# A two-layer encoder trunk on one core: which engine turns which quarter of x behind a border, and the first quarter and first weight unit in two parts

## Chip, core and metric

One core of one Trainium2 chip runs the whole kernel. The metric is the device time of one execution in microseconds, lower is better. TensorE (PE) multiplies and writes to PSUM; Vector (DVE), Scalar (ACT) and GpSimd (POOL) do the elementwise work; SyncE (SP) issues the loads.

## What is computed

Two layers on 256 tokens of width 2048 in float32: a token mixer of four head groups with one input projection `w_in` and one output projection `w_out`, and a SwiGLU with a hidden width of 5632. Each half has an RMSNorm before and behind it:

```python
def rmsnorm(x, g):
    xf = x.astype(jnp.float32)
    y = xf * lax.rsqrt(jnp.mean(xf * xf, axis=-1, keepdims=True) + EPS)
    return (y * g.astype(jnp.float32)).astype(x.dtype)

def reference(x, norm_mix_pre, ..., ffn_gate, ffn_up, ffn_down):
    split_at = np.cumsum(SPLIT_SIZES)[:-1].tolist()
    for l in range(DEPTH):
        h = rmsnorm(x, norm_mix_pre[l])
        proj = h @ w_in[l]
        a_q, a_k, a_v, b_glu, c_q, c_k, c_v, d_q, d_k, d_v = jnp.split(proj, split_at, axis=-1)
        out_a = diff_attention(a_q, a_k, a_v, diff_lambda[l], diff_subln[l], l)
        out_b = conformer_conv(b_glu, conv_dw[l], conv_dw_b[l], conv_ln_g[l], conv_ln_b[l],
                               conv_pw[l], conv_pw_b[l])
        out_c = gqa_axial_attention(c_q, c_k, c_v, gqa_q_norm[l], gqa_k_norm[l])
        out_d = neighbourhood_attention(d_q, d_k, d_v, na_rpb[l])
        mixed = jnp.concatenate([out_a, out_b, out_c, out_d], axis=-1) @ w_out[l]
        x = x + rmsnorm(mixed, norm_mix_post[l])
        h = rmsnorm(x, norm_ffn_pre[l])
        f = (jax.nn.silu(h @ ffn_gate[l]) * (h @ ffn_up[l])) @ ffn_down[l]
        x = x + rmsnorm(f, norm_ffn_post[l])
    return x
```

## The kernel before

**Products.** The 256 tokens are two halves, `tok` 0 and 1, of 128. Each projection runs over its output columns in pairs of 512-column banks and over its contraction in blocks `k` of 128 rows; for `w_in`, gate and up there are 16. One block of weights for one pair, 128x1024, is a unit. A float32 product is made of three products in a rounded format: Scalar makes the rounded high part of a unit (`whi`, `split_hi`, L222), Vector the low part, the rest (`wlo`, `split_lo`, L231), with the norm's gain taken in. The same holds for x: `xT` has a high and a low part. `products` (L297) issues, for one unit and one token half, high x high and high x low for each of the two banks, and then low x high for both: six matmuls of 512 columns. The low part of x is so needed with the fifth.

**Order.** `plan` (L261) lays the steps of a pair in groups of units; a group runs for token half 0 and then for half 1. The first pair behind a border has `FIRST` (L46), groups of 6, 5 and 5 units, the first pair of all has `START`, 2, 2, 4, 4, 4. Seven high and seven low parts may be alive (`NSPLIT`, L38), three loads of two units each (`NRAW`). The whole order is written by the program itself when it is built: `run` (L345) walks the steps, and `tick` (L318) moves generators on by one `yield` when an estimated clock of the engines says that what they wait for is done. Each engine then takes its instructions in that order.

**x at a border.** When the last bank of `w_out` or `ffn_down` is done for a token half, `post` (L494) makes the new x of that half with Vector, 512 columns (a quarter) at a time: `new_x(c)`. The next projection needs x turned: quarter `c` of x gives `xT[c]`, the blocks `k` = 4c to 4c + 3. Quarters 0 to 2 are turned by TensorE (`transpose_x`, L421): four transposes of 128x128 into one PSUM bank (`tp`, of which there are two), a high part by Scalar, a low part by Vector (`split_hi_lo`, L194). Quarter 3 is turned by Vector (L531 to L542) with 16 transposes of 32 rows by 128, in four batches with a `yield` behind each, into `xt`, from which Scalar and Vector make the parts. There are three such borders: into gate and up of layer 0, into `w_in` of layer 1, into gate and up of layer 1. At the start `first_x` (L463) has TensorE turn all quarters as they are loaded.

## Time and profile before

| | |
|---|---|
| median of 3 runs | 2178.41 us (2178.34 to 2178.55) |
| the profiled execution | 2178.1 us |
| its span in the trace | 2175.9 us |
| TensorE matmuls busy | 2154.6 us, 99% |
| Vector busy | 1300.2 us, 60% |
| Scalar busy | 1092.4 us, 50% |
| DMA | 206 GB/s mean |

The span is what the trace shows of the execution; the time has some 2 us around it. A record of a matmul is longer than its share of time, since matmuls are pipelined: the distance of two starts is the pace. Bracketed at the end of a row of the timeline is the idle time of that engine before the row and who ended it.

### The profile page before, as it was taken

The page shows a single profiled execution, that of the slowest core. Times are in us where ns is not written, and L with a number is a line of the kernel's source. Part 1 is how long each engine was busy: PE and PEld are TensorE (multiplying, and loading weights), DVE is VectorE, ACT ScalarE, POOL GpSimd, SP SyncE. Part 2 cuts the span into 40 slices and gives each one's busy share as a digit, 9 for nine tenths or more (in the row PEclk, how much of TensorE's full clock was granted, in tenths as well). Part 3 has the DMA queues.
Part 4 walks back from the last instruction along what each step waited for, and adds up shares of the span by engine and source line. Part 5 has one row for each costly group of instructions (what it writes and reads, how often), then busy time and mean ns, then how long its engine had stood idle before and what let it go on. Part 6 is the DMA issues. An engine that isn't in the chain of part 4 may idle for free.

```text
span 2175.9 us, 25246 instructions
## 1 busy us (share of the span) xinstructions
PE 2154.6 (99%) x9696; PEld 1778.7 (82%) x9696; DVE 1300.2 (60%) x1616; ACT 1092.4 (50%) x1398; POOL 29.9 (1%) x38
## 2 busy tenths in 40 slices
PE   8999999999999999999999999999999999999998
PEld 7888888888888888888878888888888888888886
DVE  5898556755546554444488974566555555454444
ACT  6656755544445444343455577555444444443432
POOL 0000000000000000000000000000000000000000
PEclk9999999999999999999999999999999999999999
DMA  7556446776776666655565563557667666665553
GB/s 277 194 176 185 170 148 223 232 219 210 225 217 220 209 226 216 220 193 193 208 225 187 193 192 136 199 188 251 213 222 223 211 215 222 222 213 213 193 219 130
DMA packets 200281, 447.52 MB, mean 206 GB/s; under 512 B 20704, under 2 KB 43744, under 8 KB 197856
## 3 DMA queue, kind: packets, MB, share of 16 engines
q1 hardware_dynamic: 200016, 445.87, 60.9%
q8 instruction: 76, 1.25, 0.2%
q14 instruction: 45, 0.37, 0.1%
q10 hardware_dynamic: 144, 0.03, 0.0%
HBM read 425.93 MB, written 19.92 MB: 205 GB/s over the span
## 4 chain that ended last, share of the span: by engine, by line
PE 95%; ACT 2%; DVE 1%; issue 1%; DMA 1%; DVEq 0%; POOLq 0%; ACTq 0%; SPq 0%
PE acc L89 91%; PE tp L89 3%; PE sc L89 1%; ACT whi L89 1%; DVE wlo L89 1%; ACT workA L89 0%; DMA lc<-in_heads_dram 0%; ACT L89 0%; DVE mx L89 0%; ACT xT L89 0%; DVE xt L89 0%; DMA x<-in_x_dram 0%; ACT conv L89 0%; ACT junk L89 0%; DVE xT L89 0%
## 5 line engine op out<-in xcount | busy, mean ns | idle before, releaser
L89 PE MATMUL acc<-whi,xT 128*128 128x512 f32 x4096 | 1292.7, 393 | 5.4 <-ACT xT L89 2.4
L89 PEld LDWEIGHTS acc<-whi,xT 128*128 128x128 f32 x4096 | 770.0, 188 | 169.5 <-ACT xT L89 3.5
L89 PE MATMUL acc<-wlo,xT 128*128 128x512 f32 x2048 | 799.4, 390 | 2.6 <-DVE wlo L89 2.6
L89 ACT ACTIVATE whi<-raw,gains 128x1024 fp32r<-128x1024 f32 x512 | 580.5, 1150 | 365.3 <-PE acc L89 334.3
L89 DVE SCALAR_TENSOR_TENSOR wlo<-raw,gains,whi 128x1024 fp32r<-128x1024 f32 x512 | 641.7, 1278 | 188.9 <-ACT whi L89 180.9
L89 PEld LDWEIGHTS acc<-wlo,xT 128*128 128x128 f32 x2048 | 385.3, 188 | 81.9 <-DVE wlo L89 4.4
L89 DVE TENSOR_TENSOR wlo<-raw,whi 128x1024 fp32r<-128x1024 f32 x240 | 292.6, 1223 | 260.5 <-ACT whi L89 243.8
L89 PE MATMUL acc<-whi,hT 128*128 128x512 f32 x1408 | 434.1, 389 | 0.0
L89 ACT ACTIVATE whi<-raw 128x1024 fp32r<-128x1024 f32 x240 | 253.7, 1061 | 304.1 <-PE acc L89 304.0
L89 PEld LDWEIGHTS acc<-whi,hT 128*128 128x128 f32 x1408 | 264.3, 188 | 55.0
L89 PE MATMUL acc<-wlo,hT 128*128 128x512 f32 x704 | 273.9, 389 | 0.0
L89 PEld LDWEIGHTS acc<-wlo,hT 128*128 128x128 f32 x704 | 132.1, 188 | 27.3
L89 DVE TENSOR_TENSOR hT<-ht,hT 128x1024 fp32r<-128x1024 f32 x22 | 27.0, 1226 | 163.5 <-ACT hT L89 163.5
L89 DVE SCALAR_TENSOR_TENSOR h<-acc,rstd,h 128x512 f32<-128x512 f32 x44 | 33.1, 751 | 113.4 <-ACT h L89 113.4
L89 DVE SCALAR_TENSOR_TENSOR conv<-uT,lc,conv 128x256 f32<-128x256 f32 x240 | 99.4, 481 | 0.0
L89 ACT ACTIVATE hT<-ht 128x1024 fp32r<-128x1024 f32 x22 | 23.3, 1059 | 128.7 <-DMA ht<-h_blocks 128.7
L89 ACT ACTIVATE h<-acc,rstd 128x512 f32<-128x512 f32 x44 | 30.3, 689 | 80.5 <-PE acc L89 80.3
L89 ACT ACTIVATE junk<-acc 128x512 bf16<-128x512 f32 x32 | 19.0, 595 | 55.9 <-PE acc L89 53.0
L89 PE MATMUL acc<-whi,mixC 128*128 128x512 f32 x128 | 44.7, 402 | 0.0
L89 DVE TENSOR_TENSOR mg<-acc,gpost 128x512 f32<-128x512 f32 x32 | 21.3, 686 | 35.8 <-PE acc L89 19.5
L89 PE MATMUL acc<-whi,mixB 128*128 128x512 f32 x128 | 42.2, 397 | 0.0
L89 PE MATMUL acc<-whi,mixD 128*128 128x512 f32 x128 | 41.6, 391 | 0.0
(139 smaller groups left out, 987.4 us busy)
## 6 DMA issues: line engine op xcount, KB each, us to landing
raw<-in_ffn_gate_dram SPq DMA_DIRECT2D x176, 512.0 KB, 3.8
raw<-in_ffn_up_dram SPq DMA_DIRECT2D x176, 512.0 KB, 5.1
raw<-in_ffn_down_dram SPq DMA_DIRECT2D x88, 1024.0 KB, 5.0
raw<-in_w_in_dram SPq DMA_DIRECT2D x63, 1024.0 KB, 5.1
raw<-in_w_out_dram SPq DMA_DIRECT2D x32, 1024.0 KB, 5.0
raw<-in_w_in_dram SPq DMA_DIRECT2D x34, 512.0 KB, 4.7
h_blocks<-blocks SPq DMA_DIRECT2D x44, 256.0 KB, 5.5
ht<-h_blocks SPq DMA_DIRECT2D x88, 128.0 KB, 6.0
```

Source lines behind the costliest of these rows:

```text
L89: return f(*args, **kw)
```

## The change

Four things. In `post` a new number `early` says how many quarters TensorE turns: 2 at a border into gate and up, 4 at the one into `w_in`. The rest, quarters 2 and 3 or none, is turned by Vector in a loop, each when the quarter before is marked; the 16 transposes are now a function `turn`. `transpose_x` takes quarter 0 in two halves with a PSUM bank for each, at the borders and at the start, and so claims both banks. `new_x(0)` is made in two halves of 256 columns. The first unit of all (`index` 0) has its high and its low part made in two pieces of 512 columns.

```diff
@@ -219,6 +219,11 @@
             self.load(self.raws[self.next_raw], between)
             self.next_raw += 1
 
+    @staticmethod
+    def pieces(u):
+
+        return [slice(0, 512), slice(512, 1024)] if u.index == 0 else [slice(0, 1024)]
+
     def split_hi(self, u):
         self.chain = 0.0
         u.hi = self.wp.tile([P, 1024], F32R, tag="hi", name=self.name("whi"))
@@ -226,7 +231,8 @@
         if gain is None:
             self.nc.scalar.activation(u.hi, w, AF.Copy)
         else:
-            self.nc.scalar.activation(u.hi, w, AF.Copy, scale=gain[:, u.k:u.k + 1])
+            for cs in self.pieces(u):
+                self.nc.scalar.activation(u.hi[:, cs], w[:, cs], AF.Copy, scale=gain[:, u.k:u.k + 1])
 
     def split_lo(self, u):
         self.chain = 0.0
@@ -235,9 +241,10 @@
         if gain is None:
             self.nc.vector.tensor_tensor(u.lo, w, hi, op=ALU.subtract)
         else:
-            self.nc.vector.scalar_tensor_tensor(
-                u.lo, w, gain[:, u.k:u.k + 1], hi, op0=ALU.mult, op1=ALU.subtract
-            )
+            for cs in self.pieces(u):
+                self.nc.vector.scalar_tensor_tensor(
+                    u.lo[:, cs], w[:, cs], gain[:, u.k:u.k + 1], hi[:, cs], op0=ALU.mult, op1=ALU.subtract
+                )
 
     def splits_to(self, n, needed):
 
@@ -421,18 +428,24 @@
     def transpose_x(self, phase, tok, c):
 
         nc = self.nc
-        yield from self.claim("tp")
+        halves = 2 if c == 0 else 1
+        n = 4 // halves
+        yield from self.claim("tp", halves)
         if tok == 0:
             self.xT[c] = self.slot([2, 4, S], F32R, "xT")
-        b = self.bank("tp", (4, P))
-        for i in range(4):
-            k = 4 * c + i
-            nc.tensor.transpose(b[:, i], self.x[tok][:, k * P:(k + 1) * P], self.ident)
-        dst = [self.xT[c][:, i, :, tok * P:(tok + 1) * P] for i in range(2)]
-        self.split_hi_lo(dst, b)
+        banks = []
+        for h in range(halves):
+            b = self.bank("tp", (n, P))
+            banks.append(b)
+            for i in range(n):
+                k = 4 * c + h * n + i
+                nc.tensor.transpose(b[:, i], self.x[tok][:, k * P:(k + 1) * P], self.ident)
+        for h, b in enumerate(banks):
+            dst = [self.xT[c][:, i, h * n:(h + 1) * n, tok * P:(tok + 1) * P] for i in range(2)]
+            self.split_hi_lo(dst, b)
         self.mark("x", phase, c, tok)
         yield
-        self.free("tp")
+        self.free("tp", halves)
 
     def x_stats(self, tok):
         for c in range(4):
@@ -514,32 +527,32 @@
                                   self.x[tok][:, c * 512:(c + 1) * 512])
             return
         yield
-        new_x(0)
+        for h in range(2):
+            cs = slice(h * 256, (h + 1) * 256)
+            nc.vector.scalar_tensor_tensor(self.x[tok][:, cs], self.mg[phase, 0][:, tok, cs], r, self.x[tok][:, cs],
+                                           op0=ALU.mult, op1=ALU.add)
         new_x(1)
         then = ("gu", phase[1]) if phase[0] == "out" else ("in", phase[1] + 1)
-        for c in range(3):
-            yield
-            self.spawn(self.transpose_x(then, tok, c))
+        early = 2 if phase[0] == "out" else 4
+        for c in range(4):
+            yield
+            if c < early:
+                self.spawn(self.transpose_x(then, tok, c))
             if c + 2 < 4:
                 new_x(c + 2)
         self.x_stats(tok)
         nc.sync.dma_start(self.xd[rows, :], self.x[tok])
         yield
         self.x_rstd(then, tok)
-        yield
-        yield from self.until(1, "x", then, 2, tok)
-        if tok == 0:
-            self.xT[3] = self.slot([2, 4, S], F32R, "xT")
-        t = self.tmp([4, P], "xt")
-        for q in range(4):
-            qs = slice(32 * q, 32 * q + 32)
-            for r in range(4):
-                rs = slice(32 * r, 32 * r + 32)
-                src = self.x[tok][:, 3 * 512:].rearrange("p (k n) -> p k n", k=4)
-                nc.vector.transpose(t[qs, :, rs], src[rs, :, qs])
-            yield
-        self.split_hi_lo([self.xT[3][:, i, :, tok * P:(tok + 1) * P] for i in range(2)], t)
-        self.mark("x", then, 3, tok)
+        for c in range(early, 4):
+            yield
+            yield from self.until(1, "x", then, c - 1, tok)
+            if tok == 0:
+                self.xT[c] = self.slot([2, 4, S], F32R, "xT")
+            t = self.tmp([4, P], "xt")
+            yield from self.turn(t, self.x[tok][:, c * 512:(c + 1) * 512])
+            self.split_hi_lo([self.xT[c][:, i, :, tok * P:(tok + 1) * P] for i in range(2)], t)
+            self.mark("x", then, c, tok)
 
 
     def ffn_half(self, phase, j, tok):
@@ -575,6 +588,16 @@
         self.split_hi_lo(dst, t.rearrange("p t (k n) -> p k t n", k=4))
         for tok in range(T):
             self.mark("h", l, j, tok)
+
+    def turn(self, dst, src):
+
+        src = src.rearrange("p (k n) -> p k n", n=P)
+        for q in range(4):
+            qs = slice(32 * q, 32 * q + 32)
+            for r in range(4):
+                rs = slice(32 * r, 32 * r + 32)
+                self.nc.vector.transpose(dst[qs, :, rs], src[rs, :, qs])
+            yield
 
 
     def layer_consts(self, l):
```

Vector, border into gate and up of layer 0. `wlo` are low parts of units, 7 to 11 here; `xt_3126` and `xt_3253` are quarter 3 of token halves 0 and 1, one row is a batch of four. Before:

```order
L89 SCALAR_TENSOR_TENSOR wlo_3155<-raw_2983,gains,whi_3132 128x1024
L89 SCALAR_TENSOR_TENSOR wlo_3177<-raw_3009,gains,whi_3153 128x1024
L89 STREAM_TRANSPOSE xt_3126<-x_2742 32x4x32 x4
L89 TENSOR_TENSOR xT_3090<-tp_3189,xT_3090 128x4x128
L89 SCALAR_TENSOR_TENSOR wlo_3198<-raw_3009,gains,whi_3175 128x1024
L89 TENSOR_REDUCE xs_3209<-ssx 128x1
L89 TENSOR_SCALAR ms_3211<-xs_3209 128x1
L89 SCALAR_TENSOR_TENSOR wlo_3216<-raw_3036,gains,whi_3196 128x1024
L89 SCALAR_TENSOR_TENSOR wlo_3226<-raw_3036,gains,whi_3214 128x1024
L89 STREAM_TRANSPOSE xt_3126<-x_2742 32x4x32 x4
L89 STREAM_TRANSPOSE xt_3253<-x_2744 32x4x32 x4
L89 TENSOR_TENSOR xT_3125<-xt_3126,xT_3125 128x4x128
```

Now, where `xt_3165` and `xt_3244` are quarter 2 of token halves 0 and 1, and `xt_3276` is quarter 3 of half 0; the first row is the low part of unit 8:

```order
L89 SCALAR_TENSOR_TENSOR wlo_3172<-raw_3021,gains,whi_3151 128x1024
L89 SCALAR_TENSOR_TENSOR wlo_3191<-raw_3021,gains,whi_3170 128x1024
L89 STREAM_TRANSPOSE xt_3165<-x_2750 32x4x32 x4
L89 SCALAR_TENSOR_TENSOR wlo_3208<-raw_3047,gains,whi_3189 128x1024
L89 SCALAR_TENSOR_TENSOR wlo_3218<-raw_3047,gains,whi_3206 128x1024
L89 TENSOR_REDUCE xs_3229<-ssx 128x1
L89 TENSOR_SCALAR ms_3231<-xs_3229 128x1
L89 STREAM_TRANSPOSE xt_3165<-x_2750 32x4x32 x4
L89 STREAM_TRANSPOSE xt_3244<-x_2752 32x4x32 x4
L89 STREAM_TRANSPOSE xt_3165<-x_2750 32x4x32 x4
L89 STREAM_TRANSPOSE xt_3244<-x_2752 32x4x32 x4
L89 TENSOR_TENSOR xT_3164<-xt_3165,xT_3164 128x4x128
```

Quarter 2 of half 0 has its last two batches behind the low parts of units 10 and 11, about where quarter 3 had its last; quarter 3 starts behind that.

TensorE, the same border: the end of unit 7 and the start of unit 8 (the first of quarter 2) for token half 0. Before:

```order
L89 MATMUL acc_3039<-whi_3132,xT_3047 128x512
L89 MATMUL acc_3040<-whi_3132,xT_3047 128x512
L89 MATMUL acc_3039<-whi_3153,xT_3090 128x512 [waits Activation_49]
L89 MATMUL acc_3039<-wlo_3177,xT_3090 128x512 [waits DVE_49]
L89 MATMUL acc_3040<-whi_3153,xT_3090 128x512
```

Now (`xT_3164` is quarter 2):

```order
L89 MATMUL acc_3050<-whi_3134,xT_3065 128x512
L89 MATMUL acc_3051<-whi_3134,xT_3065 128x512
L89 MATMUL acc_3050<-whi_3151,xT_3164 128x512 [waits Activation_49]
L89 MATMUL acc_3050<-wlo_3172,xT_3164 128x512 [waits DVE_49]
L89 MATMUL acc_3051<-whi_3151,xT_3164 128x512
```

The same product waits for Scalar in both; its `xT` came through TensorE and PSUM before and comes through Vector's `xt` now.

TensorE, border into `w_in` of layer 1: `x_7699` and `x_7701` (now `x_7739` and `x_7741`) are token halves 0 and 1. Before:

```order
L89 MATMUL acc_8057<-whi_8024,xT_8064 128x512
L89 MATMUL tp_8108<-ident,x_7699 128x128 [waits PE_49]
L89 MATMUL tp_8108<-ident,x_7699 128x128 x3
L89 MATMUL acc_8056<-whi_8033,xT_8064 128x512
L89 MATMUL acc_8056<-wlo_8052,xT_8064 128x512
L89 MATMUL acc_8057<-whi_8033,xT_8064 128x512
L89 MATMUL acc_8057<-wlo_8052,xT_8064 128x512
L89 MATMUL acc_8056<-whi_8033,xT_8064 128x512
L89 MATMUL acc_8057<-whi_8033,xT_8064 128x512
L89 MATMUL tp_8127<-ident,x_7701 128x128 [waits DMAHW6_49,DVE_49,PE_49]
L89 MATMUL tp_8127<-ident,x_7701 128x128 x3
L89 MATMUL acc_8134<-whi_7917,xT_8016 128x512 [waits Activation_49]
```

Now:

```order
L89 MATMUL acc_8100<-whi_8077,xT_8114 128x512
L89 MATMUL tp_8159<-ident,x_7739 128x128 [waits PE_49]
L89 MATMUL tp_8159<-ident,x_7739 128x128 x3
L89 MATMUL tp_8167<-ident,x_7739 128x128 [waits PE_49]
L89 MATMUL tp_8167<-ident,x_7739 128x128 x3
L89 MATMUL tp_8180<-ident,x_7741 128x128 [waits DMAHW6_49,DVE_49]
L89 MATMUL tp_8180<-ident,x_7741 128x128
L89 MATMUL tp_8183<-ident,x_7741 128x128 [waits DVE_49]
L89 MATMUL tp_8183<-ident,x_7741 128x128
L89 MATMUL acc_8190<-whi_7957,xT_8057 128x512 [waits Activation_49]
```

Quarters 2 and 3 of half 0 and quarter 0 of half 1 (in two banks) follow each other with no product between, and unit 5 stands ahead of them all.

## Rows read from the trace of the kernel before

**Rows 1.** The page, part 1: busy us, share of the span, instructions by engine.
```profile
PE 2154.6 (99%) x9696; PEld 1778.7 (82%) x9696; DVE 1300.2 (60%) x1616; ACT 1092.4 (50%) x1398; POOL 29.9 (1%) x38
```

**Rows 2.** Windows, first gate/up pair of layer 0: us, busy by engine, clock, DMA.
```profile
364.80:411.00 46.20, 45.10 (x207) 36.79 (x206) 40.77 (x71) 30.48 (x44) 3.11 (x3) 1.00 0.69 229
```

**Rows 3.** Groups by shape, whole run: count, then busy us, mean ns, idle before.
```profile
L89 DVE STREAM_TRANSPOSE xt<-x 32x128 f32<-32x128 f32 x96 | 29.0, 303 | 1.5
...
L89 DVE TENSOR_TENSOR mixD<-tp,mixD 128x256 fp32r<-128x256 f32 x8 | 3.4, 425 | 11.9 <-ACT mixD L89 11.9
...
L89 ACT ACTIVATE mixD<-tp 128x256 fp32r<-128x256 f32 x8 | 3.0, 376 | 10.4 <-PE tp L89 10.4
...
L89 ACT ACTIVATE h<-acc,rstd 128x512 f32<-128x512 f32 x44 | 30.3, 689 | 80.5 <-PE acc L89 80.3
```

**Rows 4.** Timeline, TensorE: start us, us of the record, what; last products of w_out, layer 0.
```profile
362.71 0.39 PE L89 MATMUL acc<-whi,mixD 128*128 128x512 f32 x1
...
362.94 0.60 PE L89 MATMUL tp<-ident,x 128*128 128x128 f32 x4
...
363.61 0.40 PE L89 MATMUL acc<-wlo,mixD 128*128 128x512 f32 x1
```

**Rows 5.** Timeline, start of gate and up of layer 0, all engines.
```profile
364.77 0.40 PE L89 MATMUL acc<-whi,xT 128*128 128x512 f32 x1
...
366.27 0.74 PE L89 MATMUL acc<-whi,xT 128*128 128x512 f32 x2 [0.41 <-DVE xT L89]
...
374.59 0.60 PE L89 MATMUL tp<-ident,x 128*128 128x128 f32 x4
...
375.23 0.60 ACT L89 ACTIVATE xT<-tp 128x512 fp32r<-128x512 f32 x1 [1.23 <-PE tp L89]
...
375.86 0.69 DVE L89 TENSOR_TENSOR xT<-tp,xT 128x512 fp32r<-128x512 f32 x1 [0.23 <-ACT xT L89]
...
375.88 0.50 PE L89 MATMUL acc<-whi,xT 128*128 128x512 f32 x1 [0.69 <-ACT xT L89]
```

**Rows 6.** Timeline, the same pair later on, all engines.
```profile
387.55 2.48 DVE L89 SCALAR_TENSOR_TENSOR wlo<-raw,gains,whi 128x1024 fp32r<-128x1024 f32 x2
...
390.06 2.54 DVE L89 STREAM_TRANSPOSE xt<-x 32x128 f32<-32x128 f32 x8
...
391.36 0.63 ACT L89 ACTIVATE xT<-xt 128x512 fp32r<-128x512 f32 x1 [1.06 <-DVE xt L89]
...
391.51 0.84 PE L89 MATMUL acc<-whi,xT 128*128 128x512 f32 x3
...
392.87 0.84 PE L89 MATMUL acc<-whi,xT 128*128 128x512 f32 x3
...
405.58 1.28 ACT L89 ACT_TABLE_LOAD   x1 [3.94 <-PE acc L89]
```

**Rows 7.** Waits of TensorE, 1080 to 1150 us: us in total, times, longest.
```profile
PE acc L89 <- DVE wlo L89: 2.1, 3, 0.9
```

**Rows 8.** Timeline, first pair of w_in in layer 1, TensorE.
```profile
1087.39 0.40 PE L89 MATMUL acc<-whi,xT 128*128 128x512 f32 x1
...
1133.01 0.50 PE L89 MATMUL acc<-whi,xT 128*128 128x512 f32 x1 [0.35 <-ACT xT L89]
```

**Rows 9.** Timeline, start of the run, TensorE and Vector.
```profile
7.31 0.79 PE L89 MATMUL acc<-whi,xT 128*128 128x512 f32 x1 [1.72 <-ACT whi L89]
...
8.63 0.79 PE L89 MATMUL acc<-wlo,xT 128*128 128x512 f32 x1 [0.53 <-DVE wlo L89]
...
9.74 1.28 DVE L89 SCALAR_TENSOR_TENSOR wlo<-raw,gains,whi 128x1024 fp32r<-128x1024 f32 x1 [1.17 <-ACT whi L89]
...
12.64 0.63 PE L89 MATMUL acc<-whi,xT 128*128 128x512 f32 x1
...
14.59 0.39 PE L89 MATMUL acc<-wlo,xT 128*128 128x512 f32 x1
```

## Prediction

> **What bounds the kernel now.** Read first the busy line of the page [rows 1]: TensorE is busy 99% of 2175.9 us, so the only time to be won is TensorE's own instructions or one of its few gaps. Then the stretches [rows 2]: over the first column pair behind a border into gate and up, TensorE is busy 45.10 of 46.20 us, but Vector already 40.77, 88%. That is the number to see: off the borders Vector has room, here it has 5.4 us. Last the order of time at the borders [rows 5, 6, 8], for who is late where.
>
> I call the work of one `k` for one token half a unit-step: six products. Two points one step apart, 391.51 and 392.87 [rows 6], give 1.36 us for it, 0.227 a product. Four transposes between two products cost TensorE 363.61 - 362.71 less two products, 0.90 - 0.45 = 0.45 us [rows 4].
>
> These prices carry a check. From the first gate/up product at 364.77 [rows 5] to the end of token half 0 (27 steps in FIRST's order, 36.7 us, and five groups of transposes, 2.25) is 38.95; the table load that waits for this end starts at 405.58 [rows 6], 40.8 later. So 1.85 us are lost, at the two waits of 0.41 and 0.69 that the rows show and at the restarts behind them [rows 5].
>
> **Border into gate and up, twice.** Removed: two groups of transposes on TensorE (quarter 2, both halves), 0.9 us. Split in two: the first quarter. At 366.27 TensorE waits 0.41 for the low part of quarter 0 [rows 5]; a 256-column copy on Vector takes 0.42 against 0.69 at 375.86 [rows 3, 5], so this falls to some 0.15, 0.4 with its restart. At 374.59 the transposes of token half 1 start and the product waits until 375.88 [rows 5]; with halves, Scalar starts after two transposes and its copy takes 0.38 instead of 0.60 [rows 3, 5], so some 0.45 is left.
>
> Moved: quarter 2 becomes 32 Vector transposes at 0.303 [rows 3], four of them 1.27 back to back (2.54 for eight) [rows 6], so 10.1 us more on Vector per border against 5.4 of room. Where does it land? Vector takes its instructions in order, and the order of the changed program shows where. Up to 391.32, when the last four transposes of quarter 3, half 0 end and Scalar can copy them at 391.36 [rows 6], Vector did, from the low part of quarter 0 on: nine `wlo`, four batches of four transposes, six copies of low parts, five of `x`. In the changed order the last batch of quarter **2**, half 0 stands behind nine `wlo`, four earlier batches, four low parts' worth and five of `x`: one batch more (1.27), two copies fewer (1.3), some 0.3 for halves. So the quarter that is now turned first arrives where the last one did: 391.6, Scalar's copy until 392.3 (0.63 as at 391.36).
>
> But quarter 3 was not wanted until `k` = 12; quarter 2 is wanted at `k` = 8, the fifteenth step. TensorE stands there at 364.77 + 14 x 1.36 + 3 x 0.45 + 0.9 (the two waits) = 386.1. **It waits 6.2 us.** Behind that:
> - the low part of quarter 2 follows one more batch, at 393.6, where the fifth product is due at 393.2: 0.4.
> - Quarter 3, half 0: from 391.6 Vector has eight batches, two low parts and three `wlo` (1.25 each: two from 387.55 to 390.06 [rows 6]) in front of and with it, 10.2 + 1.3 + 3.75 = 15.2, so 406.8, copied by 407.4. TensorE, nine steps on, is there at 404.95: 2.45.
> - Its low part stands behind two `wlo` and one batch: 411.2, due 408.3: 2.9.
> - Half 0 then ends at 415.7. Half 1's copy of quarter 3 now stands on Scalar behind the table load (1.28 [rows 6]) and Silu (0.69 [rows 3]), which wait for that end: 418.3, and TensorE, one step on, is there at 417.1: 1.2.
>
> Waits of 0.9 + 6.2 + 0.4 + 2.45 + 2.9 + 1.2 = 14.05, less 1.85 that go, less 0.9 of transposes: **+11.3 us**, twice +22.6. The ends: without the last two terms (they hang on two instructions' places) +7; upward +13.5, for the clock, below.
>
> One rule weighs here. Rows: a 512-column quarter costs Vector 16 x 0.303 = 4.8 us, TensorE 0.45. The Trainium skill, VectorE: DVE Perf Modes, Rules for kernel authors, says to turn 128x128 blocks on TensorE where the result may go to PSUM, and its section on the three transpose paths that Vector turns only 32x32 blocks. By that rule a border gives 10.1 us of Vector for 0.9 of TensorE and should lose; by the bound alone (TensorE 99%) it should win the 0.9 and a share of the waits. The 88% says that the rule holds here.
>
> **Border into w_in of layer 1, once.** Here Vector turns nothing any more. From 1087.39 to 1133.01 [rows 8] are 28 steps (38.1) and five groups (2.25): 5.3 of the 45.6 are lost, 2.1 of it (0.9 at most at once) at three `wlo` that stand between Vector's transposes [rows 7]. With 32 transposes fewer (9.9 us) these `wlo` are early, and the wait for quarter 3 at 1133.01 goes as well. Added: two groups, 0.9. New: three groups follow each other on two PSUM banks, so token half 1's first quarter waits until Scalar and Vector have emptied the bank of quarter 2: 0.64 to Scalar's start, 0.63 to Vector's, 0.69 for Vector [rows 5], 1.96 after that group's start; then two transposes and Scalar's half copy, some 0.85. That is 2.8, of which 1.35 is transposing: 1.5 lost, against 0.9 for the old wait there. With 0.4 and 0.2 for the first and second low part: -5.3 + 2.1 + 0.9 = **-2.3**. Ends: -4.4 (no bank wait, no other) and 0.
>
> **The start.** Scalar makes half a quarter behind two transposes and half a unit, so the first product can start some 0.7 before 7.31 [rows 9]. But the second unit's `wlo` begins at 9.74 when its high part is there, which waits for its load, and ends at 11.02 [rows 9]; neither moves. In the new order the second unit comes before token half 1's transposes, so TensorE now waits for that `wlo`; five products at the slow pace (0.43) and the transposes behind it bring half 1's second product to about 14.5, where it stands at 14.59 [rows 9]. **0**; between -0.7 (the lead is kept) and +1.2, if the clock, which rises between 12.64 and 14.59 (a product's record is 0.63, then 0.39 [rows 9], the ratio of 1.2 to 2.4 GHz, nearly), rises 2.4 us later because the last gap before it now ends at 11.05 instead of 8.63.
>
> Sum: 22.6 - 2.3 + 0 = +20.3. The profiled execution took 2178.1 (span 2175.9 and 2.2 around it), 0.3 below the median 2178.41: **2178.4 + 20.3 = 2199**.
>
> **Rivals.**
> - *The waits go and nothing replaces them.* If Vector had quarter 2 by 386.1, each gate/up border would win 1.85 + 0.9 and the other 5.3 - 0.9: 9.9 in all, **2168.5**. For it: the waits of the rows at the borders are for just these copies, and TensorE has less to do. Against: it takes 5.5 us less of Vector's time between 366.3 and 391.6, of 25, where Vector was 88% busy with the same kinds of work [rows 2, 5]. It decides as soon as the copy is there by 386.1.
> - *Only the first wait is paid.* Vector catches up while TensorE stands and quarter 3 is in time: 6.2 + 0.9 + 0.4 - 2.75 = +4.75 a border, with -2.3 **2185.6**. For it: in the wait Vector does batches of quarter 3 and of half 1 already. Against: the 15.2 of Vector's own work that is left until then, against 12.7 of TensorE's.
> - *About even*: the planner's order is late on paper only, a wait of 1 to 2 us at each border, paid by -2.3: **2176 to 2182**. Against it the same sum as in the first.
> - *The clock falls in the 6 us wait.* Rows: at the start, after waits, products took the slow record until 12.64 at least [rows 9]; the waits of the rows behind that are 0.9 at most [rows 5, 7], so none shows what one of 6 does. The slow stretch without a gap lasted from 8.63 to somewhat before 14.59 [rows 9]; half of 6.0 is 3.0 a border, but the next wait (2.45) would cover most: 0.5 to 3.0, **2200 to 2205**. The Trainium skill, TensorE: Matmul & The Clock Gate, Part 1, says that half clock is the default and that an idle TensorE goes back to it. By that rule this rival is the case, and the start of this trace agrees.
>
> **How the numbers follow.** Forecast (2190 to 2201 by itself): 0.62. Clock on top: 0.15. Only the first wait: 0.11. Waits go: 0.06. Even: 0.06. The forecast's lower end: 2 x 7 - 4.4 - 0.7 = +8.9, 2187; the upper end: 2 x 13.5 + 0 + 1.2 = +28, 2206. That leaves out the two cheap cases and part of the third. A measurement tells 0.2% (4.4 us): faster 0.06, same 0.06, slower 0.88.
>
> **What would show it.** In the profile after: in the waits of TensorE one of some 6 us for Scalar's `xT` near 386, some 20 us behind it one of about 2.5 and one for Vector's `xT`, and the same in layer 1; Vector 95% busy or more from 390 to 411; the table load at about 415.7 instead of 405.6. At the w_in border no wait for `wlo`, and one of about 1 to 2 us at the transposes of token half 1. At the start a first product near 6.6, a gap before 11.05, half 1 where it was. I am wrong if Vector's batches overlap with other work there, if quarter 2 is ready by 388, or if Scalar's copy doesn't wait for the fourth batch.

## Result, and the profile after

| | before | after |
|---|---|---|
| median | 2178.38 us (2178.15 to 2178.55, 4 runs) | 2204.54 us (2203.96 to 2205.74, 4 runs) |
| span of the profiled execution | 2175.9 us | 2202.2 us |
| mean granted TensorE clock | 0.999 | 0.993 |

The changed kernel takes 1.0121 times as long, 95% interval 1.0103 to 1.0138: 26.2 us slower, where 20.3 were forecast (2199) and the range ended at 2206.

The page's busy line, to be read against [rows 1]: us, share of the span, instructions.

```profile
PE 2163.8 (98%) x9688; PEld 1782.6 (81%) x9688; DVE 1311.2 (60%) x1663; ACT 1094.8 (50%) x1407; POOL 27.4 (1%) x38
```

TensorE has eight records fewer and yet is 9 us longer busy: products got longer. The waits of TensorE over the whole run (us in total, times, longest) say where the rest is:

```profile
PE acc L89 <- ACT xT L89: 17.0, 9, 6.6
PE acc L89 <- DVE xT L89: 5.1, 4, 2.5
...
PE tp L89 <- DVE xT L89: 1.1, 2, 1.0
```

The timeline of TensorE at the border into gate and up of layer 0 (start, us of the record, what, in brackets the idle time before it and who ended it), to be read against [rows 5, 6]:

```profile
364.40 0.40 PE L89 MATMUL acc<-whi,xT 128*128 128x512 f32 x1
...
374.48 0.50 PE L89 MATMUL acc<-whi,xT 128*128 128x512 f32 x1 [0.25 <-ACT xT L89]
...
392.73 0.79 PE L89 MATMUL acc<-whi,xT 128*128 128x512 f32 x1 [6.58 <-ACT xT L89]
393.32 0.63 PE L89 MATMUL acc<-wlo,xT 128*128 128x512 f32 x1
...
398.40 0.39 PE L89 MATMUL acc<-wlo,xT 128*128 128x512 f32 x1
...
408.36 0.50 PE L89 MATMUL acc<-whi,xT 128*128 128x512 f32 x1 [0.46 <-ACT xT L89]
...
411.91 1.60 PE L89 MATMUL acc<-whi,xT 128*128 128x512 f32 x3 [2.35 <-DVE xT L89]
413.31 0.63 PE L89 MATMUL acc<-wlo,xT 128*128 128x512 f32 x1
...
415.66 0.39 PE L89 MATMUL acc<-wlo,xT 128*128 128x512 f32 x1
...
420.77 0.50 PE L89 MATMUL acc<-whi,xT 128*128 128x512 f32 x1 [1.07 <-ACT xT L89]
```

At 392.73 quarter 2 of half 0 comes 6.58 us late. At 408.36 quarter 3 is 0.46 late, at 411.91 its low part 2.35, at 420.77 half 1's quarter 3 1.07. Behind the waits of 6.58 and 2.35 the records are 0.63 to 0.79 instead of 0.39, up to 398.40 and up to 415.66: the slow pace, at the lower of the clock's two levels.

Vector and Scalar in the same stretch:

```profile
388.23 5.06 DVE L89 STREAM_TRANSPOSE xt<-x 32x128 f32<-32x128 f32 x16
...
394.04 5.06 DVE L89 STREAM_TRANSPOSE xt<-x 32x128 f32<-32x128 f32 x16
...
411.16 0.69 DVE L89 TENSOR_TENSOR xT<-xt,xT 128x512 fp32r<-128x512 f32 x1
```

```profile
392.04 0.63 ACT L89 ACTIVATE xT<-xt 128x512 fp32r<-128x512 f32 x1 [4.21 <-DVE xt L89]
...
407.70 0.61 ACT L89 ACTIVATE xT<-xt 128x512 fp32r<-128x512 f32 x1
...
418.22 1.28 ACT L89 ACT_TABLE_LOAD   x1 [9.91 <-PE acc L89]
```

Scalar waits for Vector's transposes, TensorE for Scalar. The table load, which marks the end of half 0, is at 418.22 and not at 405.58 [rows 6]. Windows of the same stretch (us; busy by PE, PEld, DVE, ACT, POOL with records; granted clock, DMA share, GB/s):

```profile
386.00:393.00 7.00, 0.42 (x2) 0.28 (x2) 6.71 (x20) 1.78 (x2) 0.55 (x1) 0.65 1.01 385
393.00:400.00 7.00, 7.00 (x20) 5.50 (x21) 6.68 (x20) 0.63 (x1) 0.00 (x0) 0.62 0.13 50
400.00:407.00 7.00, 7.00 (x32) 5.79 (x31) 6.80 (x14) 4.98 (x5) 0.00 (x0) 1.00 0.32 99
```

Vector is busy 20.19 of these 21 us, 96%. TensorE does 20 records in 7 us in the second window and 32 in the third.

The other places, TensorE: the first product of all, the wait behind it for a low part of weights, the first product of `w_in` in layer 1 and the wait for a PSUM bank there.

```profile
6.71 0.80 PE L89 MATMUL acc<-whi,xT 128*128 128x512 f32 x1 [1.08 <-ACT whi L89]
...
10.77 0.79 PE L89 MATMUL acc<-wlo,xT 128*128 128x512 f32 x1 [0.34 <-DVE wlo L89]
...
1101.38 0.39 PE L89 MATMUL acc<-whi,xT 128*128 128x512 f32 x1
...
1112.59 0.44 PE L89 MATMUL tp<-ident,x 128*128 128x128 f32 x2 [0.98 <-DVE xT L89]
```

Marks that both traces have give the ledger. First product of gate and up, layer 0: 364.40 against 364.77, -0.4. First of `w_in`, layer 1: 1101.38 against 1087.39, so the border and its layer +14.4. First of gate and up, layer 1 (1456.93 against 1445.02): `w_in` -2.1. The end, 26.3 us later: second border +14.4.

### The profile page after: what moved, and what is told of

Same layout as the page of the kernel before. It is cut to its first block, busy times and chain, and to the rows that moved or that the text cites. A ratio compares the mean times of both kernels' runs of the same rounds, so it can differ in the third digit from the quotient of the medians.

```text
span 2202.2 us, 25286 instructions
## 1 busy us (share of the span) xinstructions
PE 2163.8 (98%) x9688; PEld 1782.6 (81%) x9688; DVE 1311.2 (60%) x1663; ACT 1094.8 (50%) x1407; POOL 27.4 (1%) x38
## 4 chain that ended last, share of the span: by engine, by line
PE 93%; DVE 4%; ACT 2%; issue 1%; DMA 0%; SPq 0%; DVEq 0%; POOLq 0%; ACTq 0%
PE acc L89 89%; PE tp L89 3%; DVE xt L89 1%; DVE wlo L89 1%; PE sc L89 1%; ACT workA L89 0%; ACT L89 0%; DVE xT L89 0%; ACT whi L89 0%; DMA raw<-in_w_in_dram 0%; DVE mx L89 0%; DVE x L89 0%; ACT xT L89 0%; ACT conv L89 0%; ACT qkD L89 0%
## 5 line engine op out<-in xcount | busy, mean ns | idle before, releaser
L89 ACT ACTIVATE whi<-raw,gains 128x1024 fp32r<-128x1024 f32 (+1 forms) x513 | 581.6, 1148 | 377.3 <-PE acc L89 353.2
L89 DVE SCALAR_TENSOR_TENSOR wlo<-raw,gains,whi 128x1024 fp32r<-128x1024 f32 (+1 forms) x513 | 641.7, 1276 | 203.7 <-ACT whi L89 195.9
```

Of the source, the lines that this page charges most:

```text
L89: return f(*args, **kw)
```

## Experiments

Each was measured beside the kernel before on the same chip (its median there 2178.1 to 2178.4 us). "Border" below is the time from the first gate/up product of layer 0 to the table load, both from the kernel's timeline:

| kernel | first product | table load | border |
|---|---|---|---|
| before | 364.77 | 405.58 | 40.8 |
| after | 364.40 | 418.22 | 53.8 |
| quarter 2 back to TensorE | 364.41 | 405.68 | 41.3 |
| the same without halves at borders | 364.20 | 405.01 | 40.8 |
| quarters 2 and 3 alone | 364.39 | 416.81 | 52.4 |
| all four on TensorE | 364.46 | 406.75 | 42.3 |
| cheap transposes | 364.47 | 407.34 | 42.9 |
| TensorE busy in the first wait | 364.21 | 418.30 | 54.1 |
| in the last wait | 364.26 | 416.52 | 52.3 |
| in both | 364.52 | 417.46 | 52.9 |

Read the same way in layer 1, the border is within 0.3 us of these, but for quarters 2 and 3 alone (52.8) and the cheap transposes (43.8).

### Where the loss is

**Quarter 2 back to TensorE**, all else as changed:

```
-        early = 2 if phase[0] == "out" else 4
+        early = 3 if phase[0] == "out" else 4
```

> The changed kernel with one number put back: at a border into gate and up TensorE turns three quarters again and Vector only the last one. The w_in border, the halves and the start stay as changed. Theory (the loss is Vector's time for the second quarter and nothing else): both 6.6 us waits and all that hangs on them go, what is left is the start's -0.4, the w_in border's -2.1 and some -0.8 at each border into gate and up from the first quarter in halves (in the trace after the first two waits there are 0.3 and 0.25 us instead of 0.41 and 0.69): 2178.4 - 0.4 - 2.1 - 1.6 = 2174.3 us. Rival (the two PSUM banks that a halved quarter claims, or the new place of the loop, cost a part of the loss): 2185 us or more, with waits of TensorE for transposes at the borders.

Measured: 2176.9 us, ratio 0.9994 (0.9985 to 1.0002). The long waits are gone, so the whole loss is the second quarter. But it is 2.6 us above the forecast, and the border is 41.3, not 40.0. TensorE, with the first quarter of half 1:

```profile
375.64 0.44 PE L89 MATMUL tp<-ident,x 128*128 128x128 f32 x2 [1.20 <-DVE xT L89]
```

A halved quarter claims both PSUM banks, and one of them still holds quarter 2 of half 0. So the rival held for a small part.

**The same without halves at the borders** (the start keeps them):

```
-        halves = 2 if c == 0 else 1
+        halves = 2 if c == 0 and phase == ("in", 0) else 1
```

and `new_x(0)` in one piece again.

> The version with quarter 2 back on TensorE, and without the first quarter in halves at the borders (the start keeps its halves and the two pieces of the first unit). Theory: with three groups of transposes per half the halves claim both PSUM banks and TensorE waits for them (four waits of 3.5 us in all in the trace with halves), which took back what they won; without them a border into gate and up is as before, and the time is 2178.4 - 0.4 - 2.1 = 2175.9 us, no wait for a bank at those borders. Rival (the halves won something all the same): 2177.5 us.

Measured: 2175.99 us, ratio 0.9991 (0.9982 to 1.0). No wait for a bank, a border of 40.8 as before, and in its place the old wait for Scalar:

```profile
375.31 0.50 PE L89 MATMUL acc<-whi,xT 128*128 128x512 f32 x1 [0.69 <-ACT xT L89]
```

With three groups of transposes the halves exchange 0.69 for 1.20. What that and its restarts amount to is the difference of the two kernels, 0.9 us by the medians and 1.7 by the two profiled executions.

**Only quarters 2 and 3 to Vector at gate and up, in the kernel before:**

```
-        for c in range(3):
+        early = 2 if phase[0] == "out" else 3
+        for c in range(4):
             yield
-            self.spawn(self.transpose_x(then, tok, c))
+            if c < early:
+                self.spawn(self.transpose_x(then, tok, c))
...
+        for c in range(early, 4):
+            ...
+            yield from self.turn(t, self.x[tok][:, c * 512:(c + 1) * 512])
```

> The kernel before with one part of the change alone: at a border into gate and up Vector turns quarters 2 and 3. Whole first quarter, whole first unit, w_in border as before. Theory: all of the loss is here. A border costs what it costs in the trace after, 14.3 us, and 0.8 more since the halves are not there: 2178.4 + 2 x 15.1 = 2208.6 us, waits of about 6.6 for Scalar's xT and 2.4 for Vector's. Rival (a part of the loss comes from the halves, which put more instructions on Scalar and Vector in front of quarter 2): 2200 us or less, the first wait shorter than 6.

Measured: 2203.16 us (2201.34 to 2205.13), ratio 1.0114 (1.01 to 1.0127): neither of the two. The loss is here, but it is 5 us less than expected, and in other places:

```profile
390.41 0.79 PE L89 MATMUL acc<-whi,xT 128*128 128x512 f32 x1 [3.71 <-ACT xT L89]
...
401.84 0.50 PE L89 MATMUL acc<-whi,xT 128*128 128x512 f32 x1 [1.92 <-ACT xT L89]
...
404.52 1.65 PE L89 MATMUL acc<-whi,xT 128*128 128x512 f32 x3 [1.03 <-DVE xT L89]
```

Without halves quarter 2 of half 0 is 3.71 late, and quarter 2 of half 1, eleven us on, late again. The border is 52.4, 1.4 less than after, and 0.9 less in layer 1. So the halves, which I had booked at -0.8 a border, cost about 1 there: the planner places Vector's transposes otherwise, and the first batch of quarter 2 starts here at 375.64 and with halves at 380.40. That this place is the cause is read from the rows; no run changes it alone. The profiled execution is the slowest of the four, 2205.13, and 1.3 us of it lie at the border into `w_in`, which this kernel leaves as it was (358.97 us from there to the next gate/up product, 357.63 before); why stays open. Vector in this kernel, then after:

```profile
375.64 1.23 DVE L89 STREAM_TRANSPOSE xt<-x 32x128 f32<-32x128 f32 x4
```

```profile
380.40 1.24 DVE L89 STREAM_TRANSPOSE xt<-x 32x128 f32<-32x128 f32 x4
```

**Only the border into w_in, in the kernel before** (the same edit with `early = 3 if phase[0] == "out" else 4`):

> The kernel before with one part of the change alone: at the border into w_in of layer 1 TensorE turns all four quarters. Theory: the three waits for low parts of weights (2.1 us) and most of the losses at quarter 3 go, against 0.9 of transposes and a wait for a PSUM bank of about 1: -2 us, 2176.4. Rival (the three groups of transposes in a row cost as much as the waits were): 2178.4, and the gain after came from the halved quarter.

Measured: 2176.15 us, ratio 0.9991 (0.9982 to 1.0). As the theory has it, though the interval ends at no change. From the first product of `w_in` in layer 1 to that of gate and up the trace has 355.9 us, where before has 357.6 and after 355.6: 1.8 gained alone, 2.1 with halves.

**TensorE turns everything** (`early = 4` in the changed kernel):

> The changed kernel with all four quarters turned by TensorE at every border, so Vector turns nothing. Theory: Vector was in time with one quarter, so against the version with three quarters on TensorE (2174.3 forecast) each border into gate and up pays 0.9 us of transposes and about 1 for a PSUM bank, as the w_in border does now: 2178 us. Rival (Vector with one quarter still held TensorE up by more than that): 2172 us or less.

Measured: 2178.89 us, ratio 1.0002 (0.9994 to 1.0011). The time is the one forecast, in part by luck: the fourth quarter was to add 3.7 us to a kernel of 2174.3, and it adds 2.0 to one of 2176.9. The border is 42.3, 1.0 more than with three quarters on TensorE.

### What the loss is made of

**A quarter of Vector's time for the same order:**

```
-            qs = slice(32 * q, 32 * q + 32)
-            for r in range(4):
-                rs = slice(32 * r, 32 * r + 32)
-                self.nc.vector.transpose(dst[qs, :, rs], src[rs, :, qs])
+            self.nc.vector.transpose(dst[:, q], src[:, q])
```

(the planner is charged as before, so each engine's order is the same).

> The changed kernel, every instruction in its place, but each batch of four 32x128 transposes is one 128x128 instruction that turns the blocks without moving them to other partitions: a quarter of Vector's time for it, some 0.3 instead of 1.27 us a batch. Part of the computation is so left out (the blocks stand in the wrong place). Theory (Vector's time for the transposes is what TensorE waits for): five batches stand in front of the first late copy, so it comes 4.8 us earlier, and the wait at quarter 2 falls from 6.6 to about 1.8; the waits at quarter 3 go. A border then costs -0.5 instead of +14.3: 2178.4 - 0.4 - 2.1 - 1 = 2175 us. Rival (the place in the order, what the batches stand behind, is the cause and not their time): the copy stays within 1 us of where it is, 2200 us or more.

Measured: 2185.59 us, ratio 1.0034 (1.002 to 1.0048). The border falls from 53.8 to 42.9 (from 53.7 to 43.8 in layer 1), so 10 to 11 of the 13 us are Vector's time for the transposes. The forecast of 2175 was still 10 us too low. First the group of the cheap transposes by shape (count, busy us, mean ns, idle before), then TensorE at quarter 2 in both layers, and Vector:

```profile
L89 DVE STREAM_TRANSPOSE xt<-x 128x128 f32<-128x128 f32 x32 | 8.2, 288 | 0.0
```

```profile
388.74 0.50 PE L89 MATMUL acc<-whi,xT 128*128 128x512 f32 x1 [2.53 <-ACT xT L89]
...
1471.21 0.50 PE L89 MATMUL acc<-whi,xT 128*128 128x512 f32 x1 [3.42 <-ACT xT L89]
```

```profile
384.68 2.48 DVE L89 SCALAR_TENSOR_TENSOR wlo<-raw,gains,whi 128x1024 fp32r<-128x1024 f32 x2 [1.31 <-ACT whi L89]
```

Vector, no longer full, now stands 1.31 us for the high part of a unit with the last batches behind it in its order. So a part of the rival is true: the place of these batches leaves a border 2 to 3 us longer than before, and a faster Vector gives back only what lies behind it. The waits of 0.46 for quarter 3 and 1.07 for half 1's quarter 3, behind the table load, were left too, which I had struck out. The trace is of one of two executions at 2183 us, and in it the clock stays up behind the waits of 2.53 and 3.42 (granted 1.00 from 386 to 420 and from 1465 to 1500). The other three took 2185.6 to 2186.8, with a mean granted clock of 0.997 to 0.998 instead of 0.999; 0.001 to 0.002 of 2185 us is 2.2 to 4.4, so there the clock probably fell behind such a wait, which no trace shows.

**TensorE kept busy through the first wait, through the last one, through both:**

```
+    def keep_busy(self, n):
+        b = self.bank("sc")
+        for _ in range(n):
+            self.tc.nc.tensor.matmul(b, self.xT[0][:, 0, 0, 0:P], self.last_hi[:, 0:512], start=True, stop=True)
...
     def products(self, s):
...
+        if s.phase[0] == "gu" and s.pair == 0 and s.tok == 0 and u.k == 8:
+            self.keep_busy(26)
         for b in s.banks:
...
+        if s.phase[0] == "gu" and s.pair == 0 and s.tok == 0 and u.k == 12:
+            self.keep_busy(9)
         for b in s.banks:
```

The 26 stand ahead of the first product of quarter 2, the 9 ahead of low x high of unit 12.

> The changed kernel with 26 products of no use on TensorE (into a PSUM bank that nobody reads) ahead of the first product of quarter 2 at each border into gate and up, 5.9 us where TensorE otherwise stands still for 6.6. Theory: the clock then does not fall, the products behind have records of 0.39 instead of 0.79, but quarter 3 comes from Vector when it did, so the wait there grows from 0.46 to 3 us or so and nothing is won: 2204.5 us, within 1.5. Rival (the slow products are paid in full, 3 us a border): 2198.5 us.

Measured: 2204.07 us, ratio 1.012 (1.0105 to 1.0135), as the theory has it. TensorE:

```profile
385.79 6.05 PE L329 MATMUL sc<-whi,xT 128*128 128x512 f32 x26
392.57 0.50 PE L89 MATMUL acc<-whi,xT 128*128 128x512 f32 x1 [0.72 <-ACT xT L89]
...
407.93 0.50 PE L89 MATMUL acc<-whi,xT 128*128 128x512 f32 x1 [2.39 <-ACT xT L89]
...
411.76 1.65 PE L89 MATMUL acc<-whi,xT 128*128 128x512 f32 x3 [2.53 <-DVE xT L89]
```

The clock stays up (granted 1.00 from 386 to 407), the products behind 392.57 are fast, and what they win is waited for at quarter 3, 2.39 instead of 0.46. The clock falls behind that wait instead, and the low part of quarter 3 is used when it was, 411.76 against 411.91. The first slow stretch costs nothing.

> The changed kernel with 9 products of no use on TensorE, 2.0 us, in the wait of 2.35 us for the low part of quarter 3 at each border into gate and up. Theory: this is the last wait of the half, nothing behind it takes up time, so the slow products behind it (9 products in 3.75 us instead of 2.04) are lost in full: keeping the clock up wins 1.7 us a border, 2201.1 us. Rival (the slow stretch has another cause than standing still): the same slow records, 2204.5 us.

Measured: 2200.85 us, ratio 1.0106 (1.0091 to 1.0121), 3.7 us below the changed kernel by the medians and 3.2 by the profiled executions, where 3.4 were expected.

```profile
409.30 2.21 PE L329 MATMUL sc<-whi,xT 128*128 128x512 f32 x9
411.80 0.97 PE L89 MATMUL acc<-whi,xT 128*128 128x512 f32 x3 [0.29 <-DVE xT L89]
412.60 0.40 PE L89 MATMUL acc<-wlo,xT 128*128 128x512 f32 x1
```

The low part comes when it came (411.80 against 411.91), the records behind it are 0.40 instead of 0.63, and the border is 52.3 instead of 53.8. The second slow stretch is paid in full.

> The changed kernel with both fillings, 26 products of no use ahead of quarter 2 and 9 in the wait for the low part of quarter 3. Theory: the first wins nothing, the second 1.7 us a border, 2201.1 us, and what is then left over the kernel before, 22.7 us and 2.5 of gains elsewhere, is waiting for Vector alone. Rival (both slow stretches are paid): 2195 us.

Measured: 2201.95 us, ratio 1.011 (1.0095 to 1.0125), 1.1 above the run with the last filling alone.

```profile
408.21 0.50 PE L89 MATMUL acc<-whi,xT 128*128 128x512 f32 x1 [2.38 <-ACT xT L89]
...
409.27 0.63 PE L89 MATMUL acc<-wlo,xT 128*128 128x512 f32 x1
409.70 3.35 PE L331 MATMUL sc<-whi,xT 128*128 128x512 f32 x9
412.88 0.84 PE L89 MATMUL acc<-whi,xT 128*128 128x512 f32 x3
```

With the first wait filled TensorE is earlier at quarter 3 and stands 2.38 us there. The granted clock is 1.00 to the end of that wait and 0.50 from 408.7 to 412.1, so the nine products of no use run at the slow pace, and the next that counts starts at 412.88, a microsecond after the low part is there.

### A cheaper way for Vector, by way of DRAM

Since Vector's time is the price, quarters 2 and 3 were turned as the kernel turns h: one block transpose, a write to DRAM, four reads.

```
+    def by_dram(self, phase, tok, c):
...
+        nc.vector.transpose(b.rearrange("p q (k n) -> p k q n", k=4),
+                            self.x[tok][:, c * 512:(c + 1) * 512].rearrange("p (k q n) -> p k q n", k=4, q=4))
...
+        nc.sync.dma_start(d[rows, :], b.rearrange("p q m -> p (q m)"))
+        for _ in range(4):
+            yield
...
+        for q in range(4):
+            nc.sync.dma_start(t[32 * q:32 * q + 32], d[rows, q * P:(q + 1) * P].rearrange("(t p) m -> p t m", p=32))
+        for _ in range(4):
+            yield
...
+        self.split_hi_lo(dst, t.rearrange("p t (k n) -> p k t n", k=4))
+        self.mark("x", phase, c, tok)
```

> The changed kernel, but quarters 2 and 3 at a border into gate and up are turned as the kernel turns h: one 128x512 block transpose on Vector (0.70 us), a write to DRAM and four reads that put the 32x32 blocks on their partitions. For a half quarter of 4.8 us on Vector it takes 0.7. Theory (Vector's time was the price, and TensorE gains what it no longer turns when the copy is in time): the write and the read take 5.5 and 6.0 us from issue to landing for h, so quarter 2 of half 0, whose x is there at some 370, is copied at about 385 and TensorE, there at 386, does not wait. A border into gate and up then gains the 0.9 us of two groups of transposes and some 0.8 of the first waits: 2178.4 - 0.4 - 2.1 - 3.4 = 2172.5 us. Rival (the way through the queue is too long, or the loads of weights behind these DMAs come late): a wait of 2 to 6 us for Scalar's xT at quarter 2 or for weights, 2178 to 2190 us.

Measured: 2218.73 us, ratio 1.0185 (1.0171 to 1.0199). Missed. The data of quarter 2 had landed at 380.67, but the copies stood too early in Scalar's order, ahead of the first quarter of half 1. Scalar, then TensorE:

```profile
387.28 0.63 ACT L89 ACTIVATE xT<-xt 128x512 fp32r<-128x512 f32 x1 [5.97 <-DMA xt<-x_blocks]
387.81 0.64 ACT L89 ACTIVATE xT<-tp 128x256 fp32r<-128x256 f32 x2
```

```profile
388.23 0.79 PE L89 MATMUL acc<-whi,xT 128*128 128x512 f32 x1 [13.32 <-ACT xT L89]
```

The second try puts the planner's clock in the place of the yields:

```
-        for _ in range(4):
-            yield
+        yield from self.later(6.0)
...
-        for _ in range(4):
-            yield
+        yield from self.later(5.0)
```

> The version that turns quarters 2 and 3 by way of DRAM, with the read and the copies of the high and low part put later in the order (the read 6 us behind the write, the copies 5 us behind the read, by the planner's clock). In the trace of the first try the turned quarter had landed by 380.67 us for half 0, before TensorE wants it at 386; what cost 13.3 us at each border was that Scalar's copy stood too early in Scalar's order, 7 and 6 us ahead of its data, with the first quarter of half 1 behind it. Theory: with the copies behind the first quarters of half 1 Scalar does not stand, quarter 2 is there by 383 and a border into gate and up gains the 0.9 us of transposes and some 0.8 of the first waits: 2178.4 - 0.4 - 2.1 - 3.4 = 2172.5 us. Rival (the queue of loads: the loads of weights that now stand behind writes and reads come late): waits for whi or wlo at units 11 to 15, 2177 us or more.

Measured: 2193.72 us, ratio 1.0073 (1.0059 to 1.0086). Missed, but quarter 2 of half 0 is in time now; one long wait a border is left, for quarter 2 of half 1 (in layer 1 it is 8.05):

```profile
401.56 0.80 PE L89 MATMUL acc<-whi,xT 128*128 128x512 f32 x1 [6.82 <-ACT xT L89]
```

The third orders the transfers anew:

```
-        yield from self.later(6.0)
+        yield from self.later(16.0 if c == 3 else 1.0 if tok else 6.0)
...
-        yield from self.later(5.0)
+        yield from self.later(10.0 if c == 2 and tok else 5.0)
```

and the spill of x behind a delay of 12.

> As the version before by way of DRAM, with the DMAs in the order in which TensorE wants the quarters: the read of quarter 2 of half 1 right behind its write, quarter 3 read 16 us behind its write by the planner's clock, and the spill of x 12 us later. In the trace of the version before, quarter 2 of half 0 was in time, and one wait of 6.8 us a border was left, for quarter 2 of half 1, whose read stood behind three loads of weights and the read of quarter 3 until 393.07. Theory (that read's place is all that is left): its copy now comes at some 391, before TensorE is there at 394.7, and the wait with the slow products behind it, some 9 us a border, goes: 2193.7 less 2 x 9 to 10, 2174 to 2176 us. Rival (loads of weights are pushed back instead): waits for whi or wlo of 2 us or more a border, 2180 us or more.

Measured: 2199.12 us, ratio 1.0099 (1.0082 to 1.0116). Missed: now both halves of quarter 2 are in time and both of quarter 3 late, half 0 by 4.47 and half 1, at 416.09, by 2.97. TensorE, and a window of the stretch ahead:

```profile
403.31 0.79 PE L89 MATMUL acc<-whi,xT 128*128 128x512 f32 x1 [4.47 <-ACT xT L89]
```

```profile
390.00:400.00 10.00, 8.84 (x40) 6.98 (x38) 4.37 (x4) 3.98 (x4) 0.00 (x0) 1.00 0.99 344
```

The DMA engines are busy 99% of these 10 us: loads of weights, the spill of x, which I had moved there, and the reads of quarter 3 in one place. Vector is down to 4.37 of 10. Quarter 3 of half 0 was read by DMAs issued from 392.96 on, and Scalar's copy, which waits for them, starts at 402.63: here the transfers are what is late. For half 1 the read itself is issued only at 406.99. That an order exists in which this way wins was not shown; the three tries were slower than before.

No version beat the kernel before by more than the measurement tells. The lowest, 2175.99 and 2176.15, lie 2.1 and 2.2 us under it, with intervals that end at 1.0.

## Why the prediction was right, and where it was not

The time lies in the range and the mechanism is the one forecast. The size of a gate/up border was off by 3.1 us, twice; with 0.2 at `w_in` and -0.4 at the start that is 6.0, the span's 26.3 against 20.3. (The medians, against a rounded 2199, make it 5.5.) Its steps, us of waiting or of late start at the border of layer 0:

| step | forecast | after |
|---|---|---|
| first low part and half 1's first product | 0.9 | 0.3 and 0.25, with restarts 1.2 |
| quarter 2, half 0 | 6.2 | 6.58 |
| its low part | 0.4 | none |
| quarter 3, half 0 | 2.45 | 0.46 |
| its low part | 2.9 | 2.35 |
| half 1's quarter 3, behind table load and Silu | 1.2 | 1.07 |
| slow products behind the waits | 0, a rival | 2.75 and 1.7 |
| a border, net | +11.3 | +14.4 |
| `w_in` border | -2.3 | -2.1 |
| start | 0 | -0.4 |

The slow products are counted so: 54 products take 15.0 us from 392.73 to 407.74, which at 0.227 each would be 12.3, and 26 take 7.6 from 411.91 to 419.54 instead of 5.9. The column can be added up by distances of starts, since the brackets leave out some 0.17 at each wait: 1.2, 6.75, 0.62, 2.52 and 1.23 of waits, 2.75 and 1.73 of slow products and 0.2 of restarts (the first products behind a wait start further apart) are 17.0; less the 1.85 and the 0.9 that went, 14.3.

**Right.** Vector, 88% busy [rows 2], did not have the second quarter in time, as forecast: the first wait was sized by counting Vector's instructions in its order, and it is 0.4 off. The wait at quarter 3 was sized as well: with the clock kept up by the first filling it is 2.39, where 2.45 was forecast. Back on TensorE the quarter costs nothing (the first experiment); with a quarter of Vector's time 10 to 11 of 13 us go. The rule cited from the Trainium skill, VectorE: DVE Perf Modes, Rules for kernel authors, to turn 128x128 blocks on TensorE where PSUM will do, holds here: three quarters on TensorE 2176.9 us, two 2204.54. Only the last quarter, wanted latest, is no loss on Vector: all four on TensorE take 2178.89.

**The step that failed is the clock.** It stood as a rival of 0.15, because no wait of the trace before was longer than 0.9 behind the start [rows 5, 7]. It was part of what happened, and its time, 2200 to 2205, is the one that came, which is luck in part: its 0.5 to 3.0 a border were meant for the first wait, and that costs nothing. Its working held for one half only: that the next wait covers the slow products behind the first one is what the first filling shows, with 2.39 of waiting at quarter 3 instead of 0.46. But I priced only the 6 us wait and forgot that the wait for the low part of quarter 3, 2.9 in my own sum, is one too, and the last: nothing behind it takes up the 1.7 us. The last filling gives 1.55 a border back in the traces. The Trainium skill, TensorE: Matmul & The Clock Gate, Part 1, says that an idle TensorE goes back to half clock. The trace agrees, granted 0.65 and 0.62 around the first wait, and that rule should have had more than 0.15.

**The rest of the 3.1** is Vector again, some 1.2: quarter 3 was forecast to be copied by 407.4, 42.6 us behind the first product, and its product starts 44.0 behind it; its low part 46.4, and it starts 47.5 behind it. Vector's 15.2 us of work between the two quarters took 15.7 (392.04 to 407.70, Scalar's two copies), the first copy was 0.4 later, and all of it started 0.4 us sooner.

**Halves.** Booked, with the restarts, as 1.85 down to 0.9 a border; it is 1.2, and the waits themselves fell from 0.41 and 0.69 [rows 5] to 0.3 and 0.25. But with two quarters on Vector the kernel without halves has the shorter border (52.4 against 53.8), and with one quarter they cost a wait for a bank of 1.20. What they give, I took from the waits; what they take, two banks at once (1.20, measured) and very likely a moved order, I left out.

**w_in border.** The three waits for `wlo` [rows 7] went, the bank wait is 0.98 and 0.16 where I put 1.5: -2.1 for -2.3.

**Start.** First product at 6.71 instead of 7.31 [rows 9], the gap before 11.05 there as described (0.34 at 10.77), but 0.4 us of the lead survive. This is at the edge: the first gate/up product lies at 364.2 to 364.5 in the eleven traces with the new start, and at 364.4, 364.8 and 365.1 in the three with the old. The two overlap, so that the start wins anything there is not shown.

## What to carry to other kernels

Before work is moved from the bound engine to one that has room on average, count what stands in that engine's order between the data and the moment the result is wanted; 60% busy over the run was 88% in this stretch, and 0.9 us saved on TensorE cost 14 a border. Price every wait of TensorE in the new order that is longer than those the old trace shows together with the slow products behind it, and ask of each whether a later wait takes them up: here only the slow products behind the last one were paid.

## What the runs showed of the hardware

The granted clock fell, from 1.00 to 0.50, in or just behind waits that follow busy stretches. In the changed kernel it fell within the wait of 6.58 us (20 records in the next 7 us, fast again at 398.40) and at the end of the one of 2.35 (fast again at 415.66, 3.75 us later). It fell half a microsecond to one behind the ends of three others in this layer: 2.38 (both fillings), 2.39 (the first filling) and 1.92 (quarters 2 and 3 alone). Waits of 0.98 at `w_in` and 1.07 behind the table load left it up, and so did those of 2.53 and 3.42 in the profiled execution of the cheap kernel. So the length of a wait alone does not tell whether the clock falls. Products that nobody reads kept it at 1.00 through the first wait; where they ran at the slow pace, nine of them took 3.2 us instead of 2.0.

A 128x128 block transpose on Vector takes 288 ns, a 32x128 one 303 [rows 3] and a 128x512 one, the kernel's own for h, 706. A quarter of the partitions takes as long as all of them, so the 16 pieces that move blocks across partitions are what makes a quarter cost 4.8 us.
